# Nine adaLN products, one convolution tile, pooled sums, last squares and the last stores moved in a hybrid decoder step

## The chip, the cores and the metric

One core of one Trainium2 chip runs the whole program. The metric is the device time of one execution in microseconds (us), as the median of several runs. The engines are TensorE (PE; PEld is its loading of weights), VectorE (DVE), ScalarE (ACT), GpSimd (POOL) and SyncE (SP), which issues most of the DMAs. Each engine runs its own instructions strictly in the order in which they stand in its queue; semaphores order engines against each other.

## The reference, cut to what matters

The computation is one inference step of two layers over 1088 tokens: 1024 of a new sequence and 64 of eight running ones (eight tokens each, the "samples"). Everything is float32, the model is 1024 wide.

```
mod = silu(c) @ ada_w[i] + ada_b[i]           # adaLN: shift, scale, gate, each 1024 wide, 9 conditions
hn  = rmsnorm(x, norm_g[i]) * (1 + scale) + shift
layer 0 (SSD):  z, xbc, dt = split(hn @ w_in)             # 6176 columns
    xbc = silu(bias + causal convolution of width 4)      # x, B, C; 8 groups of 4 heads
    per chunk of 128 tokens: y = (C B^T * decay) xdt + C h * decay ;  h = decay * h + B^T xdt
    out = rmsnorm_per_group((y + d * x) * silu(z)) @ w_out
layer 1 (pool): u, z = split(hn @ w_in)                   # 2048 + 2048 columns
    pooled = windowed mean of u (2, 4, 8 or 16 tokens) - u
    out = (pooled @ w_group * scale * silu(z)) @ w_out
x = x + (1 + gate) * out                      # after each layer
y = rmsnorm(x, final_norm_g)
```

Outputs are y and the new states (SSD states, last convolution rows, last pooling rows).

## The kernel before

**Data and products.** Activations lie transposed, 128 features on the partitions and 1088 tokens beside each other, in SBUF slots that are taken and freed by hand. A float32 product is done as three products of rounded halves: `hi` = the rounded copy (ScalarE), `lo` = the rest (VectorE), and TensorE adds hi*hi, hi*lo and lo*hi (`mm1`, L190 to L192). So each weight needs a split on both engines before TensorE can use it. Weights come as a stream in a fixed list (`items`), with three raw buffers (`wr`) and two pairs of split buffers (`wh`, `wl`). `stream_next` hands out the next weight, splits the one after it and loads the following ones; raw items in between, with no split, are the adaLN weights.

**adaLN.** One adaLN block (`ada_block`, L251 to L273) is eight products of 32 columns, packed four beside each other (`am`, L261), a copy on ScalarE (`mp`) and two small selecting products one step later (L270), whose result two small VectorE instructions turn into shift and scale or gate. The first eight stand in the front stage. Fourteen more (`ada_plan`) go beside the SSD stage, and two later.

**The SSD stage** (L1587 on). Eight scans, one per group g, are cut into steps by generators, and a second generator (`beside`) yields units of projection or output products; the table `FILL` says how many units follow each scan step. Scans 0 to 3 have one unit after each of twelve steps. The steps of a scan are two fronts (transposes, C B^T), four pairs of a state step (`states`, products `S`, L623) and a row step (`rows`, products `y`, L645 and L649), where the last row step is preceded by the products Z of the samples with their old states (L664, 32 columns), then the samples' output (`back_sample`, L678), the samples' state products (`state_sample`, L700, S over 32 rows, in PSUM buffers S, y, y and tr), and the gate. The norm's sums over a group (`ms`, L763, 32 columns) and the scaling by the norm (L775) run inside the next scan, at its steps 0 and 3 (`rest`).

The units of a projection group are four weight tiles (ii = 0 to 3: B, C and two of x) of three token chunks each (c = 0 to 2). The adaLN block of a tile is opened and closed after chunks 1 and 2 for ii = 1 and 3, and after chunks 0 and 1 for ii = 2. A finished tile goes through `conv_tile`: one scaled copy on ScalarE, three taps on VectorE (L368), a tanh and two gating instructions. The last group projected is group 6, and its tile ii = 3 goes by k instead of by chunks, so that layer 0's inputs (`hn`) are freed early for the first splits (`gh`, `gl`, L805 and L806) of the output product. The first output tile (`op_first`) uses the high halves first and the low halves at its end (L835).

**The pooling layer** (L1689 on). The first two pairs of u and z tiles are plain products (`plain_pairs`, L970). Beside them `act_sums` forms sums and differences of halves of the layer's input and splits them into T1 to T4 (L1005 on ScalarE, L1006 on VectorE). The other fourteen pairs use seven products of half size instead of eight (`fast_pair`, order B11, B21, T2, T3, T1, T4, B22), with weight combinations from `w_sums`, each half split by `split_half` (L182, L184). `u_pool` forms a window's sum by repeated shifted addition (L930). After the mixing come the output products over seven block combinations in the order 2, 6, 3, 5, 1, 4, 7 (`out_product`); `block_steps` prepares the blocks of the next one (splits at L1225 and L1226, written as `b`). During product 4 the squares of finished x halves go into `ss` (L1785, L1786), and during product 7 the final norm is computed quarter by quarter, scaled (L1803 on GpSimd, L1805 on VectorE) and stored (L1806).

**What sets the order.** The program is written in the intended order, and a scheduler may bring an instruction forward on an engine when its inputs are expected earlier. `issue_after(ins)` forbids that: on the engine of `ins`, what is written in the block stands behind `ins` in the queue. It is order only, no wait between engines. The places that the change touches are of this kind, or move whole calls.

## Time and profile before

| | before |
|---|---|
| median of three runs | 1587.53 us (1587.14 to 1587.76) |
| the profiled execution's own time | 1586.18 us |
| its span | 1584.0 us |
| TensorE busy | 1568.2 us, 99% |
| VectorE busy | 1302.7 us, 82% |
| ScalarE busy | 790.8 us, 50% |
| GpSimd busy | 528.4 us, 33% |
| granted TensorE clock | 0.998 |

The profile is of one execution. Its span runs from the first to the last recorded instruction; the metric counts 2.2 us more around it. Matmuls are pipelined: the start of each is measured and its end is modelled, so two matmuls that overlap in the table are one step apart in fact, and a small wait may show as an overlap that is missing and not as idle time. "Busy" therefore says that TensorE always had something, not that it never waited.

### The profile page before, as it was taken

The numbers are of one execution on the slowest core, as the hardware profiler recorded it, in microseconds if no ns is written. First come the engines' busy times: TensorE is split into PE (matmuls) and PEld (weight loads), VectorE is DVE, ScalarE is ACT, GpSimd is POOL, SyncE is SP. The second block draws the span as 40 slices with busy tenths as digits, with TensorE's granted clock in tenths as the row PEclk, the third lists the DMA queues.
The fourth block names the chain that finished last, engine by engine and source line by source line (L and its number), as shares of the span: only waits on it lengthen the run. The fifth ranks groups of instructions, "written<-read, shape, count | busy, mean of one in ns | idle before, by whom it ended". The sixth has DMA issues, their size and how long they took to land.

```text
span 1584.0 us, 30719 instructions
## 1 busy us (share of the span) xinstructions
PE 1568.2 (99%) x11946; PEld 1504.7 (95%) x11946; DVE 1302.7 (82%) x2152; ACT 790.8 (50%) x1512; POOL 528.4 (33%) x558
## 2 busy tenths in 40 slices
PE   9999999999999999999999999999999999999997
PEld 7899999999999899989999999999999999999997
DVE  6874789887899999889888858998889777667886
ACT  6663344466666666665456338533333233233364
POOL 0133556522322413221211242576566530000241
PEclk9999999999999999999999999999999999999999
DMA  9422232355555565678999432232333379565783
GB/s 357 167 102 92 89 113 75 113 186 177 172 165 174 171 198 159 220 256 297 332 340 316 161 134 64 83 126 98 117 116 115 105 252 364 140 180 178 165 168 124
DMA packets 122304, 275.57 MB, mean 174 GB/s; under 512 B 18192, under 2 KB 59312, under 8 KB 122160
## 3 DMA queue, kind: packets, MB, share of 16 engines
q1 hardware_dynamic: 117840, 259.79, 47.9%
q0 software_dynamic: 4032, 12.72, 4.7%
q8 instruction: 94, 1.54, 0.4%
q10 hardware_dynamic: 288, 1.11, 0.2%
q14 instruction: 50, 0.41, 0.1%
HBM read 201.12 MB, written 70.23 MB: 171 GB/s over the span
## 4 chain that ended last, share of the span: by engine, by line
PE 89%; DVE 5%; issue 3%; DMA 2%; ACT 1%; POOL 0%; SPq 0%; DVEq 0%; ACTq 0%; POOLq 0%
PE st L1079 11%; PE st L1080 11%; PE st L1078 11%; PE mm L190 11%; PE mm L191 11%; PE mm L192 11%; PE op L1298 3%; PE op L1299 3%; PE op L1297 3%; PE y L645 2%; PE S L623 2%; PE y L649 2%; PE tr L584 1%; PE am L261 1%; PE tr L581 1%
## 5 line engine op out<-in xcount | busy, mean ns | idle before, releaser
L1080 PE MATMUL st<-hh,w 128*128 128x272 f32 x832 | 240.2, 289 | 0.0
L1078 PE MATMUL st<-hh,w 128*128 128x272 f32 x832 | 240.0, 289 | 0.0
L1079 PE MATMUL st<-hl,w 128*128 128x272 f32 x832 | 240.0, 288 | 0.0
L1080 PE MATMUL st<-t,w 128*128 128x272 f32 x624 | 179.6, 288 | 0.5 <-DVE w L184 0.5
L1079 PE MATMUL st<-t,w 128*128 128x272 f32 x624 | 179.3, 287 | 0.4 <-DVE t L1006 0.4
L1078 PE MATMUL st<-t,w 128*128 128x272 f32 x624 | 179.6, 288 | 0.0
L190 PE MATMUL mm<-hh,wh 128*128 128x368 f32 (+1 forms) x528 | 178.9, 339 | 0.0
L191 PE MATMUL mm<-hl,wh 128*128 128x368 f32 (+1 forms) x528 | 174.0, 330 | 0.0
L192 PE MATMUL mm<-hh,wl 128*128 128x368 f32 (+1 forms) x528 | 173.3, 328 | 0.0
L1078 PEld LDWEIGHTS st<-hh,w 128*128 128x128 f32 x832 | 156.8, 188 | 0.0
L1079 PEld LDWEIGHTS st<-hl,w 128*128 128x128 f32 x832 | 156.7, 188 | 0.0
L1080 PEld LDWEIGHTS st<-hh,w 128*128 128x128 f32 x832 | 156.4, 188 | 0.0
L182 ACT ACTIVATE w<-wr 128x512 fp32r<-128x512 f32 x104 | 65.0, 629 | 165.2 <-PE st L1080 136.2
L631 POOL TENSOR_TENSOR hd<-h,cd 128x256 f32<-128x256 f32 x56 | 46.1, 823 | 290.4 <-DVE h L632 138.4
L1297 PE MATMUL op<-b,w 128*128 128x272 f32 x448 | 129.4, 289 | 0.0
L1298 PE MATMUL op<-b,w 128*128 128x272 f32 x448 | 128.9, 288 | 0.4 <-DVE b L1226 0.4
L1299 PE MATMUL op<-b,w 128*128 128x272 f32 x448 | 129.0, 288 | 0.0
L190 PE MATMUL mm<-gh,wh 128*128 128x368 f32 (+1 forms) x372 | 125.3, 338 | 0.0
L192 PE MATMUL mm<-gh,wl 128*128 128x368 f32 (+1 forms) x372 | 122.3, 329 | 0.0
L191 PE MATMUL mm<-gl,wh 128*128 128x368 f32 (+1 forms) x372 | 122.0, 328 | 0.1
L1080 PEld LDWEIGHTS st<-t,w 128*128 128x128 f32 x624 | 117.3, 188 | 0.7 <-DVE w L184 0.7
L1079 PEld LDWEIGHTS st<-t,w 128*128 128x128 f32 x624 | 117.2, 188 | 0.6 <-DVE t L1006 0.6
(310 smaller groups left out, 4603.1 us busy)
## 6 DMA issues: line engine op xcount, KB each, us to landing
wr<-win SPq DMA_DIRECT2D x48, 512.0 KB, 3.8
wr<-pin SPq DMA_DIRECT2D x32, 512.0 KB, 3.7
acb<-acd SPq DMA_DIRECT2D x60, 256.0 KB, 5.1
wr<-pout SPq DMA_DIRECT2D x28, 512.0 KB, 3.8
x<-x1d SPq DMA_DIRECT2D x24, 544.0 KB, 6.3
x1d<-x SPq DMA_DIRECT2D x22, 544.0 KB, 4.5
wr<-pout POOLq DMA_DIRECT2D x20, 512.0 KB, 5.6
x<-xT SPq DMA_DIRECT2D x16, 544.0 KB, 8.1
```

Source lines behind the costliest of these rows:

```text
L182: self.last_hi = self.nc.scalar.activation(hi, src, AF.Copy)
L190: nc.tensor.matmul(ps[:, :n], hi[:, k, :], ah[:, a:a + n], start=first, stop=False)
L191: nc.tensor.matmul(ps[:, :n], hi[:, k, :], al[:, a:a + n], start=False, stop=False)
L192: nc.tensor.matmul(ps[:, :n], lo[:, k, :], ah[:, a:a + n], start=False, stop=last)
L623: nc.tensor.matmul(S[:, 256 * i:256 * i + 256], Bt, xde.rearrange("p r q -> p (r q)"), start=True, stop=True)
L631: nc.gpsimd.tensor_tensor(out=hd, in0=h[-1], in1=cd.unsqueeze(2).to_broadcast([P, 4, 64]), op=ALU.mult)
L1078: nc.tensor.matmul(ps[c][:, :QUART], hi[:, k], xh[:, t], start=(k == 0), stop=False)
L1079: nc.tensor.matmul(ps[c][:, :QUART], hi[:, k], xl[:, t], start=False, stop=False)
L1080: nc.tensor.matmul(ps[c][:, :QUART], lo[:, k], xh[:, t], start=False, stop=(k == 3))
L1297: nc.tensor.matmul(ps[:, :QUART], hi[:, k], xh, start=k == 0, stop=False)
L1298: nc.tensor.matmul(ps[:, :QUART], hi[:, k], xl, start=False, stop=False)
L1299: nc.tensor.matmul(ps[:, :QUART], lo[:, k], xh, start=False, stop=k == 7)
```

## The change

The change moves work between places and queues; all products stay. In its parts:

- adaLN blocks for ii = 2 open after chunk 2 of their tile and close after chunk 0 of the next tile; those for ii = 3 open after chunk 0 of the next group's first tile and close after its chunk 1. The stream's list puts the weights of the latter behind that tile's weight, and one more raw load is asked for at ii = 3.
- Group 6, tile ii = 2: taps 2 and 3 of the convolution, the tanh and the gating go behind the evictions of `back_sample`; the weight split at ii = 3 goes behind the eviction of the rows.
- The second weight pair of the output product is split behind the last `gh` and `gl`. In scan 5 the scaling by the norm (`rest`) goes from step 3 to step 4.
- Plain products: the first split of T goes behind the last weight's `hi` on ScalarE; the z tile of the second pair uses PSUM buffer tr for its first chunk. The first pooled sum's first addition goes behind the sixth half weight's low half, its second behind the last T split; for the second pooled sum the bound falls away.
- Squares in product 4 go behind the last block's split so far, on both engines.
- In the last quarter three squares are added into `ss` on VectorE and one stays for TensorE (four before). The last eight tiles are stored one by one, by turns from SP and ScalarE, in the order 5, 7, 0, 4, 1, 2, 6, 3 (four stores of two tiles from SP before).

```diff
...
                 lo = self.wp.tile([P, 8, P], F32R, tag="wl", bufs=2, name=self.name("wl"))
-            self.nc.scalar.activation(hi[:, :nk, :], raw[:, :nk, :], AF.Copy)
+            self.w_hi = self.nc.scalar.activation(hi[:, :nk, :], raw[:, :nk, :], AF.Copy).ins
...
         eng = self.nc.gpsimd if n > 6 and n % 7 in POOLW else self.nc.vector
-        eng.tensor_tensor(out=lo, in0=src, in1=hi.bitcast(F32), op=ALU.subtract)
+        self.lows.append(eng.tensor_tensor(out=lo, in0=src, in1=hi.bitcast(F32), op=ALU.subtract).ins)
...
         nc.scalar.activation(acc[:, :n], raw[:, :n], AF.Identity, bias=self.cwh[:, 128 + ti:129 + ti], scale=w[0])
+
+        def tap(k):
+            nc.vector.scalar_tensor_tensor(out=acc[:, :n], in0=raw[:, k:k + n], scalar=w[k], in1=acc[:, :n], op0=ALU.mult, op1=ALU.add)
+
+        def close():
+            nc.scalar.activation(raw[:, :n], acc[:, :n], AF.Tanh)
+            nc.vector.scalar_tensor_tensor(out=dst[:, :NP], in0=raw[:, :NP], scalar=1.0, in1=acc[:, :NP], op0=ALU.add, op1=ALU.mult)
+            th, v = (t[:, 1027:1115].rearrange("p (b w) -> p b w", w=11)[:, :, 0:8] for t in (raw, acc))
+            nc.vector.scalar_tensor_tensor(out=dst[:, NP:TOK].rearrange("p (b i) -> p b i", i=8), in0=th, scalar=1.0, in1=v, op0=ALU.add, op1=ALU.mult)
+
+        if ti == 2 * BESIDE[-1]:
+            with self.tc.issue_after(self.row_evict):
+                tap(1)
+            self.taps_late = lambda: [tap(k) for k in (2, 3)], close
+            return
         for k in range(1, 4):
-            with self.tc.issue_after(self.row_evict) if k == 1 and ti == 2 * BESIDE[-1] else contextlib.nullcontext():
-                nc.vector.scalar_tensor_tensor(out=acc[:, :n], in0=raw[:, k:k + n], scalar=w[k], in1=acc[:, :n], op0=ALU.mult, op1=ALU.add)
-        nc.scalar.activation(raw[:, :n], acc[:, :n], AF.Tanh)
-        nc.vector.scalar_tensor_tensor(out=dst[:, :NP], in0=raw[:, :NP], scalar=1.0, in1=acc[:, :NP], op0=ALU.add, op1=ALU.mult)
-        th, v = (t[:, 1027:1115].rearrange("p (b w) -> p b w", w=11)[:, :, 0:8] for t in (raw, acc))
-        nc.vector.scalar_tensor_tensor(out=dst[:, NP:TOK].rearrange("p (b i) -> p b i", i=8), in0=th, scalar=1.0, in1=v, op0=ALU.add, op1=ALU.mult)
+            tap(k)
+        close()
...
         for ii in range(4):
-            w = self.stream_next()
+            with self.tc.issue_after(self.row_evict) if (G["g"], ii) == (BESIDE[-1], 3) else contextlib.nullcontext():
+                w = self.stream_next()
+            if ii == 3 and (G["g"], 3) in self.ada_plan:
+                self.stream_raw(self.wpos + 2)
...
                         self.slots.free(*self.hn[j])
+                    if k == 0:
+                        next(self.ada_open[2], None)
...
                 return
-            ada = self.ada_do(self.ada_plan[G["g"], ii]) if (G["g"], ii) in self.ada_plan else iter(())
+            if (G["g"], ii) in self.ada_plan:
+                self.ada_open[ii] = self.ada_do(self.ada_plan[G["g"], ii])
...
                 self.proj_evict(G, ii, raw, ps, c, (G["g"], ii) != (BESIDE[-1], 2))
-                if c != (0, 0, 2, 0)[ii]:
-                    next(ada, None)
+                ada = {(1, 1): 1, (1, 2): 1, (2, 2): 2, (3, 0): 2, (0, 0): 3, (0, 1): 3}.get((ii, c))
+                if ada in self.ada_open:
+                    next(self.ada_open[ada], None)
...
                     nc.tensor.matmul(py[o, :64], xz[:, r, :], M[:, r, :64], start=True, stop=True)
-                evac_y(py, q, tok, 64)
+                evac = evac_y(py, q, tok, 64)
+            if self.taps_late:
+                taps, close = self.taps_late
+                with self.tc.issue_after(evac):
+                    taps()
+                close()
+                self.taps_late = None
...
             m -= step
-            with self.tc.issue_after(self.t_last) if p < PLAIN and step == 1 else contextlib.nullcontext():
+            with self.tc.issue_after({1: self.lows[5], 2: self.t_new}[step]) if p == 0 and step < 4 else contextlib.nullcontext():
...
         def z_tile(p, w, c, ch):
-            ps = self.pp.tile([P, 512], F32, tag="tr", bufs=2, name=self.name("pl")) if p == c == 0 else self.plain_tile(1 if p == 0 else c)
+            ps = self.pp.tile([P, 512], F32, tag="tr", bufs=2, name=self.name("pl")) if c == 0 else self.plain_tile(1 if p == 0 else c)
...
         def split(x, hi, lo):
-            nc.scalar.activation(hi, x, AF.Copy)
+            with self.tc.issue_after(self.w_hi) if not self.T else contextlib.nullcontext():
+                nc.scalar.activation(hi, x, AF.Copy)
...
             t = sl.get("t", F32R)
+            split(x, t[:, h1], t[:, h2])
             self.T[i, k] = t
-            split(x, t[:, h1], t[:, h2])
+            self.t_new = self.t_last
...
-        self.nsplit = 0
+        self.nsplit, self.lows = 0, []
...
         self.ada_late = dict(zip([(0, 4), (0, 6)], ada[len(places):]))
+        self.ada_open = {}
...
                 items.append((io["win"][6 * g + ii], 8))
-                if (g, ii) in self.ada_plan:
-                    items += self.ada_items(self.ada_plan[g, ii])
+                at = (BESIDE[BESIDE.index(g) - 1], 3) if ii == 0 and g != BESIDE[0] else (g, ii)
+                if at in self.ada_plan and (ii < 3):
+                    items += self.ada_items(self.ada_plan[at])
...
         self.acts = [[] for _ in PARTS]
-        self.zadd = None
+        self.zadd = self.taps_late = None
...
                         next(rest, None)
-                    elif i == 3 and j == 0:
+                    elif i == 3 + (g == 5) and j == 0:
...
             if d % 2 == 0:
-                ws = self.stream_pair()
+                with contextlib.ExitStack() as behind:
+                    for ins in (self.op_hi, self.op_lo) if p + d == 0 else ():
+                        behind.enter_context(self.tc.issue_after(ins))
+                    ws = self.stream_pair()
...
-        def scale(a, n, ps, groups, pool):
+        def scale(a, n, ps, groups, pool, queues=()):
...
                         nc.vector.scalar_tensor_tensor(out=t[:, i], in0=o, scalar=fg, in1=ps[:, :n], op0=ALU.mult, op1=ALU.mult)
-                nc.sync.dma_start(io["yT"][ks[0]:ks[-1] + 1][:, :, a:a + n].rearrange("k p n -> p k n"), t)
+                    if queues:
+                        queues[i % 2].dma_start(io["yT"][k][:, a:a + n], t[:, i])
+                if not queues:
+                    nc.sync.dma_start(io["yT"][ks[0]:ks[-1] + 1][:, :, a:a + n].rearrange("k p n -> p k n"), t)
...
         def squares(d, c):
-            if d and c == 0:
-                square(d, HALF, HALF)
-            if d < 3 and c == 1:
-                square(4 + d, HALF, HALF)
+            with self.tc.issue_after(self.last_block[0]), self.tc.issue_after(self.last_block[1]):
+                if d and c == 0:
+                    square(d, HALF, HALF)
+                if d < 3 and c == 1:
+                    square(4 + d, HALF, HALF)
...
         ws = ws[24:]
-        sq, sqs = [], sl.get("sq")
+        sqs = sl.get("sq")
...
                 else:
-                    t = sqs[:, QUART * d:QUART * d + QUART]
-                    nc.scalar.activation(t, x[d][:, a:a + QUART], AF.Square)
-                    sq.append(t)
+                    if d < 3:
+                        square(d, QUART, QUART)
+                    else:
+                        nc.scalar.activation(sqs[:, :QUART], x[d][:, a:a + QUART], AF.Square)
...
                             scale(0, QUART, p, ((4, 5, 6, 7), (0, 1, 2, 3)), (0, 4))
-        p1 = norm(QUART, QUART, sq)
-        scale(QUART, QUART, p1, ((4, 5), (6, 7), (0, 1), (2, 3)), (4, 6))
+        p1 = norm(QUART, QUART, [sqs])
+        scale(QUART, QUART, p1, ((5, 7, 0, 4), (1, 2, 6, 3)), (4, 6), (nc.sync, nc.scalar))
...
```

## Rows read from the trace of the kernel before

**Rows 1.** The page's busy times: us, share of the span, instructions of each engine.
```profile
PE 1568.2 (99%) x11946; PEld 1504.7 (95%) x11946; DVE 1302.7 (82%) x2152; ACT 790.8 (50%) x1512; POOL 528.4 (33%) x558
```

**Rows 2.** Stretches: from:to, length, busy PE, PEld, DVE, ACT, POOL, clock, DMA, GB/s.
```profile
481.00:553.00 72.00, 72.00 (x573) 65.79 (x572) 64.34 (x96) 48.40 (x109) 20.54 (x31) 1.00 0.54 176
...
1011.40:1053.00 41.60, 40.68 (x322) 40.24 (x321) 40.01 (x60) 15.43 (x30) 22.78 (x18) 1.00 0.40 139
```

**Rows 3.** Waits of TensorE: who, for whom: us in total, times, longest.
```profile
PE st L1080 <- DVE w L184: 0.5, 1, 0.5
...
PE st L1079 <- DVE t L1006: 0.4, 1, 0.4
PE op L1298 <- DVE b L1226: 0.4, 1, 0.4
PE pl L192 <- DVE wl L145: 0.3, 1, 0.3
```

**Rows 4.** Order of time, TensorE in op_first: start, length, what, count, idle before.
```profile
708.10 0.43 PE L835 MATMUL mm<-gl,wh 128*128 128x368 f32 x1 [0.37 <-DVE gl L806]
709.30 1.60 PE L835 MATMUL mm<-gl,wh 128*128 128x368 f32 x8 [0.77 <-DVE gl L806]
```

**Rows 5.** Order of time, TensorE around two adaLN blocks (am).
```profile
443.42 1.07 PE L261 MATMUL am<-wr,scp 128*32 128x256 f32 x16
444.42 0.44 PE L645 MATMUL y<-M,xd 128*64 128x128 f32 x4
...
759.98 1.07 PE L261 MATMUL am<-wr,scp 128*32 128x256 f32 x16
760.87 0.40 PE L664 MATMUL Z<-h,ctm 128*32 128x256 f32 x4
```

**Rows 6.** Order of time, state products of scans 1 and 4, eviction of scan 4.
```profile
482.83 0.51 PE L700 MATMUL S<-xs,Bt 32*128 32x512 f32 x4
...
696.69 1.09 PE L700 MATMUL S<-xs,Bt 32*128 32x512 f32 x4
...
695.48 0.27 DVE L615 SCALAR_TENSOR_TENSOR xbc<-xbc,vec,y 128x64 f32<-128x64 f32 x1
```

**Rows 7.** Order of time, VectorE before the last gl.
```profile
705.62 1.22 DVE L145 TENSOR_TENSOR wl<-wr,wh 128x1024 fp32r<-128x1024 f32 x1
```

**Rows 8.** Order of time in scan 5, VectorE and TensorE.
```profile
731.29 1.34 DVE L775 SCALAR_TENSOR_TENSOR xbc<-xbc,vec,rs 128x1088 f32<-128x1088 f32 x1
...
734.33 0.39 PE L645 MATMUL y<-M,xd 128*64 128x128 f32 x4
734.86 0.44 PE L649 MATMUL y<-ea,h 128*64 128x128 f32 x4
```

**Rows 9.** Order of time in the plain products, ScalarE, then VectorE.
```profile
992.03 1.75 ACT L1005 ACTIVATE t<-x 128x544 fp32r<-128x544 f32 x3
996.95 0.66 ACT L1005 ACTIVATE t<-x 128x544 fp32r<-128x544 f32 x1 [3.17 <-DVE x L1002]
997.51 1.04 ACT L141 ACTIVATE wh<-wr 128x1024 fp32r<-128x1024 f32 x1
...
1016.42 1.43 DVE L930 TENSOR_TENSOR ws<-u 128x1222 f32<-128x1222 f32 x1
```

**Rows 10.** Order of time in product 4, VectorE.
```profile
1547.79 0.73 DVE L1786 TENSOR_TENSOR ss<-ss,sq 128x544 f32<-128x544 f32 x1
1548.43 0.73 DVE L1226 TENSOR_TENSOR b<-gin,b 128x544 fp32r<-128x544 f32 x1
```

**Rows 11.** Order of time in the tail, TensorE, ScalarE, VectorE, store issues (SPq).
```profile
1573.86 2.00 PE L304 MATMUL ms<-sq,ones 128*128 128x272 f32 x8
...
1574.14 0.43 ACT L1843 ACTIVATE sq<-x 128x272 f32<-128x272 f32 x1 [1.97 <-DVE x L1282]
...
1576.85 2.54 DVE L1805 SCALAR_TENSOR_TENSOR y<-x,vec,ms 128x272 f32<-128x272 f32 x6 [2.74 <-ACT ms L1792]
...
1578.14 2.20 SPq L1806 DMA_DIRECT2D yT<-y  x4
```

**Rows 12.** GB/s of the DMAs from 1575 to 1584, in 40 slices.
```profile
GB/s 0 0 0 0 0 0 0 0 0 0 0 0 0 0 0 0 0 24 329 372 314 358 319 348 343 305 372 377 368 368 372 334 49 0 0 0 0 0 0 0
```

## The prediction

> **What bounds the kernel now.** I read the page's busy times first, then the stretches, then who waits for whom on TensorE, and last the order of time at each wait. TensorE is busy 1568.2 of the 1584.0 us span [rows 1], and a whole group of the SSD stage shows it busy 72.00 of 72.00 us [rows 2]. So no other engine's time counts as such. What can be won is of three kinds: waits of TensorE, the extra time where its tiling changes (products over 32 or 64 columns beside products over 128), and the tail behind the last product. The waits are few and short: 0.5 and 0.4 us in the pooling layer's first pair, 0.4 in the last layer's blocks, 0.3 in the plain products [rows 3]. These are idle times behind a modelled end; from start to start a wait costs more. Two low-half products start 1.20 us apart where the row gives 0.77 idle and the usual step is 0.17 (eight in 1.60, the last one's 0.43 included) [rows 4]: 1.03 lost, 0.26 more than the idle. I add 0.2 to each idle of rows 3 for that, an estimate. All the edits lie at such places, so their sum is some microseconds of 1584, and the sign is easier to tell than the size.
>
> **The change part by part** (us, against the profiled execution; minus is a gain).
>
> *Nine adaLN products moved.* No product is added or removed. Five blocks (ii = 2) go from before a scan's rows to before its sample products Z, four (ii = 3) from before the state products S to before the norm's sums one group on. A block before rows takes 1.00 from its start to that of the next product (443.42 to 444.42); the one block that stands before Z already takes 0.89 (759.98 to 760.87) [rows 5]. Z and the norm's sums both use 32 columns, so I take 0.11 for each: 9 x 0.11 = -1.0. Bounds: 0, if the product behind pays the change of tiling itself, and -1.4, if the norm's sums also save their own entry (another 0.1 on four, an estimate of the same size). Each block's two selecting products, its copy on ScalarE and its two small sums on VectorE move with it; VectorE idles 7.7 in those 72 us [rows 2]. Each block also has two weight loads on SP, and the next group's first weight now waits in SP's queue for the buffer that the moved block frees. It is needed three steps later, 18 us at 12 steps in 72 [rows 2], so I cost it at nothing; without that cover TensorE would wait for the rest of the load and for the splitting, 1.04 on ScalarE and 1.22 on VectorE [rows 7, 9], in each of four groups.
>
> *Convolution of group 6, rows before weights, second weight pair behind the last split.* Before, the sample output's eviction starts only at 695.48, behind long convolution taps, and the state products take 1.09 where the same four take 0.51 in another group [rows 6]: -0.6. The new order puts two taps behind the evictions. Then `op_first` waits for the low halves `gl`, idle 0.37 and 0.77 [rows 4], while VectorE spent 1.22 on a weight's `wl` just before them [rows 7]; the new order puts this `wl` behind both. The two gains are not independent: VectorE's queue is full here, and the end of the last `gl` sets the second wait. It comes 1.22 sooner for the `wl` and little sooner for the taps, which only change places. So both together give at least 1.2 if the queue stays as it is, and at most 0.6 + 1.5 (0.37 + 0.77 + 0.4) = 2.1; I take -1.3, near the lower end, since the queue is the nearer row. What now waits behind `wl`, the gate's second half and the norm's sum of scan 4, comes no later than before, as the `gl` leave 1.22 earlier; if one tap more gets between, the norm's sums wait, up to +0.7 (half a tap pair's 1.4, an estimate). The weight itself is wanted six products later, group 6's inputs two scans on.
>
> *Scan 5's two scalings by the norm, one step later.* Two quads of row products start 0.53 apart at 734.33, and a quad itself takes 0.39 with its drain [rows 8]; I take a usual step of 0.2, so -0.3. The state sum that they wait for is queued behind scalings of 1.34 each. These, 2.7 together, then come behind the next state sums and one unit, and evictions queue behind them; two y buffers cover that. Bounds -0.4 and +0.4 (the same wait, one step on).
>
> *Plain products and pooled sums.* Gains: the waits for the last plain weight (0.3 + 0.2), for the first pair's weight (0.5 + 0.2) and for a T half (0.4 + 0.2) [rows 3], 1.8 if all go. The last two queue on VectorE behind a pooled sum of 1.43 at 1016.42 [rows 9] and its second step; both now go behind a later weight and a later T half. The z tile in another PSUM buffer takes away a wait for an eviction, 0 to -0.3, counted as 0. Against it: the first three splits of T on ScalarE, from 992.03, now stand behind the weight's `hi`, which ran at 997.51 for 1.04. ScalarE idled 3.17 before 996.95 [rows 9]. If the `hi` runs at the start of that idle time, the splits begin at 996.95 - 3.17 + 1.04 = 994.8, 2.8 late; if it runs where it did, at 998.55, 6.5 late. I take the early place and count on VectorE forming other differences of x meanwhile, as half of them need no split; of the 2.8 I let 0.6 reach TensorE. Sum -1.2; bounds -2.1 and +7.8 (6.5, and two deferred sums of 1.43, less the 1.6 that VectorE idles in the first two pairs [rows 2]).
>
> *Last squares behind the last block's halves.* A sum of squares at 1547.79 stands ahead of a block's low half on VectorE, and the next block takes the slot that this low half frees [rows 10]; TensorE idles 0.4 for it [rows 3]: -0.6 with the 0.2. The sum comes back between there and the first norm; bounds -0.6 and +0.7 (its 0.73, if the norm's sums wait for it).
>
> *Tail.* The products over the last squares, eight matmuls, take 2.00 to 1575.86; the last square is there at 1574.14 + 0.43 = 1574.57 [rows 11]. With three of the four squares added up on VectorE, two matmuls are left behind it, one step of 0.2 and one with its drain, 0.4: 1575.2, so -0.6. Stores: before, four of two tiles each, the first issued at 1578.14, and then some 14 slices of 0.225 us at about 350 GB/s without a gap [rows 12]. The first of the six products that start at 1576.85 and take 2.54 [rows 11] is done at about 1577.3; its own store can go then, 0.8 earlier. The same bytes at the same rate end as much earlier, unless the last product, at 1579.39, holds the end; then its store is shorter by a tile of 139 KB (128 x 272 x 4 bytes), 0.4 at that rate. I take -0.5, bounds 0 and -0.8. Together -1.1.
>
> The Trainium skill (DMA: Bandwidth & Descriptors, "Issuing engines are not separate DMA queues") says that transfers of several issuing engines run interleaved on the same 16 DMA engines, so that a second issuing engine saves only the time of issuing. By this rule the second queue gives nothing once the data flow without a gap; the trace agrees, since one queue alone held 350 GB/s. By the same page ("Anatomy of one DMA") a DMA costs about 2.0 us fixed, whatever its size, and by that the stores would end 0.4 sooner and not 0.5.
>
> **Sum.** -1.0 - 1.3 - 0.3 - 1.2 - 0.6 - 1.1 = -5.5. The profiled execution took 1586.18 (the span and 2.2 around it) and would take 1580.7. The median of the runs is 1587.53, 1.35 more, and the new runs are read by their median too: 1587.5 - 5.5 = 1582.0.
>
> **The rivals.**
> *Part of it only.* A wait that goes is followed by the next late operand on the same full queue. For it: VectorE is busy 40.01 of 41.60 us in the first pairs [rows 2], and two gains have merged into one already. Against it: where VectorE idles 7.7 of 72, TensorE has no wait. Then adaLN, half the tail and a third of the other 3.4: -1.0 - 0.55 - 1.1 = -2.65, 1584.9.
> *It does not do what it says.* The new edges bind order alone; where an operand is late for a load or a buffer, the wait stays. For it: ScalarE, too, idled before it ran the weight's `hi`. Then -1.0 remains and one new wait of 0.6: 1587.1.
> *Slower.* The last plain weight's `hi` holds back the first T splits by the full 6.5, the pair's T products come late, the pooled sums fall into the next pair, and VectorE cannot make it up: +7.8 in place of -1.2, with the other -4.3 that is +3.5, 1591.0. It decides from a lateness of 3.0 on, if nothing fills VectorE meanwhile: 3.0 + 2.9 - 1.6 = 4.3, which eats the rest. Against it: that `hi` would have to run no earlier than it did.
>
> **How the numbers follow.** The forecast has 0.58 (its own range 1579.8 to 1584.3), part of it 0.23, nothing 0.10, slower 0.09. A measurement of this kernel can tell about 0.2%, 3.2 us, from no change, so faster is below 1584.4: nearly all of the forecast, 0.55, and four tenths of the second case, 0.09, together 0.64. Slower is above 1590.7: about half of the last case, 0.05. The rest, 0.31, is neither. The range for 8 in 10 begins at 1579.2, where the larger gains come near their upper bounds, and ends at 1587.2, which takes in the second case and half of the third.
>
> **What would show it.** The ii = 2 blocks stand directly before Z and take 0.89, the ii = 3 blocks before the norm's sums. The state products of scan 4 take 0.5, and the low-half products of `op_first` wait under 0.4. Scan 5's rows have no step of 0.5. The first T split starts by 995, and TensorE does not wait in the first pair. No block wait near 1550. Eight stores; two products over squares behind the norm's two instead of eight. The forecast is wrong if new waits stand between 1011 and 1053, if a row or state product waits in scans 1 to 4, or if the span is within 1 us of 1584.

## The result: slower, 1592.02 us

The changed kernel takes 1592.02 us (median of seven runs, 1591.38 to 1594.46) against 1587.14 beside it (1586.19 to 1588.12), a ratio of 1.0032, 95% interval 1.0022 to 1.0042. I had said 1582.0, and 1579.2 to 1587.2 as the range. Its profiled execution took 1592.34, with a span of 1590.6.

The page after: TensorE is as full as before [rows 1], and the work has not grown.

```profile
PE 1569.3 (99%) x11940; PEld 1508.1 (95%) x11940; DVE 1298.1 (82%) x2155; ACT 800.4 (50%) x1520; POOL 517.3 (33%) x558
```

The waits of TensorE after; the columns are who waits, for whom, us in total, times, the longest. Of [rows 3] both `st` waits and the `op` wait are gone, as forecast (the last by luck, as the squares below show). New are six waits of state products `S` for `xd`, four short ones of the samples' `S`, and the `pl` wait has grown from 0.3 to 2.9.

```profile
PE S L641 <- DVE xd L618: 4.6, 6, 2.1
PE pl L192 <- DVE wl L145: 2.9, 1, 2.9
...
PE S L724 <- DVE xbc L633: 0.7, 4, 0.2
```

**Where the time went.** I take the start of one and the same TensorE product in both traces and subtract (a plus: later than in the kernel before). The columns are the product's time in the kernel before: ahead of the scans, samples' `S` of scan 4, products `Z` of scan 5, norm's sums of scan 7 (898.46), last plain product, 2400th half product, first product of the output stage, its last one, end. The first column is from execution to execution; what counts are differences along a row. Even these carry the execution: e8 and e12 have the same instructions in the same order on every engine up to 950, and e12 alone has a wait of 0.7 ahead of the first output product. The experiments' rows come from their profiled executions in the same way.

```
                      343.4  696.7  760.9  898.5 1011.4 1061.2 1403.1 1573.3 1584.0
changed               -0.38   3.49   1.92   5.10   9.94   8.49   8.48   7.58   6.57
e1  adaLN undone      -0.04   0.22   0.70   2.49   7.48   6.03   6.02   5.12   4.11
e2  scan 5 undone     -0.36   4.53   3.61   3.61   5.80   5.75   5.74   4.83   3.82
e3  T order undone    -0.71   3.37   1.80   3.92   3.88   3.44   3.43   2.55   1.55
e4  all three undone   0.11   0.03   1.08   1.08   1.06   0.63   0.62  -0.29  -0.73
e5  adaLN alone        0.11   4.05   2.08   2.08   2.08   2.08   2.08   1.56   1.58
e6   + other bank      0.17   2.97   2.02   2.02   1.93   1.93   1.92   1.33   1.35
e7   + evict first    -0.49   0.95  -0.07  -0.07  -0.06  -0.03  -0.04  -0.70  -0.70
e8   + both           -0.76  -0.50  -2.55  -2.55  -2.63  -2.60  -2.61  -3.39  -3.38
e9  conv. alone       -0.52  -0.05  -0.20  -0.10  -0.13  -0.11  -0.12  -0.41  -0.40
e10 pair alone        -0.64   0.12   4.20   4.20   4.17   4.18   4.16   3.49   3.49
e11 changed + copy    -0.24   3.57   2.20   2.82   4.88   4.79   4.77   4.29   3.29
e12 best              -0.61  -0.21  -1.54  -1.54  -1.64  -2.07  -2.08  -2.82  -3.83
e13 T order + sums    -0.47  -0.69  -0.61  -0.61   3.08   1.63   1.61   1.11   1.11
e14 sums alone         0.05   0.09   0.65   0.65   0.70   0.25   0.24  -0.46  -0.45
```

The changed kernel loses 3.9 in scans 0 to 3, gains 1.6 to 760.9, loses 3.2 in scan 7 and 4.8 in the plain products, then gains 1.5, 0.9 and 1.0.

**Scans 0 to 3, first wait.** TensorE and VectorE of the changed kernel at the samples of scan 0 (start, duration, engine, line, operation, tiles, count, idle before and its releaser):

```profile
409.43 0.49 PE L724 MATMUL S<-xs,Bt 32*128 32x512 f32 x2
410.10 0.50 PE L724 MATMUL S<-xs,Bt 32*128 32x512 f32 x2 [0.18 <-DVE xbc L633]
```

```profile
408.03 0.26 DVE L633 SCALAR_TENSOR_TENSOR xbc<-xbc,vec,y 128x64 f32<-128x64 f32 x1
408.49 1.23 DVE L372 SCALAR_TENSOR_TENSOR xbc<-raw,raw 128x1024 f32<-128x1024 f32 x1 [0.20 <-ACT raw L371]
409.63 0.22 DVE L374 SCALAR_TENSOR_TENSOR xbc<-raw,raw 128x64 f32<-128x64 f32 x1
409.77 0.28 DVE L633 SCALAR_TENSOR_TENSOR xbc<-xbc,vec,y 128x64 f32<-128x64 f32 x1
```

The second pair of `S` starts 0.67 behind the first (0.01 is usual) and at the end of the second eviction, 410.05, which frees its PSUM buffer. The waits table shows only 0.2 of this as idle. The same places in the kernel before:

```profile
409.65 0.46 DVE L615 SCALAR_TENSOR_TENSOR xbc<-xbc,vec,y 128x64 f32<-128x64 f32 x2
```

```profile
410.20 1.07 PE L261 MATMUL am<-wr,scp 128*32 128x256 f32 x16
411.20 0.51 PE L700 MATMUL S<-xs,Bt 32*128 32x512 f32 x4
```

The second eviction ended no earlier there, at 410.11, and `S` began behind the block, at 411.20. But the block was not needed for that: the two evictions stand together there, and the second ends 0.09 ahead of the block's start (0.08 in scans 1 and 3; in scan 2 it ends 0.33 behind it). What is new is VectorE's order. In the kernel before the gating stands behind both evictions, at 411.23; in the changed kernel it is ready earlier, and its 1.23 and 0.22 stand between them. By these rows the block's 1.0 would have covered that (409.43 + 1.00 is behind 410.05), but with the old order its absence would have cost at most 0.33, in scan 2.

**Second wait.** At the next scan's start, changed kernel (TensorE, then VectorE):

```profile
419.26 1.07 PE L261 MATMUL am<-wr,scp 128*32 128x256 f32 x16
420.15 0.64 PE L787 MATMUL ms<-z,ones 128*32 128x272 f32 x8
...
426.43 0.38 PE L602 MATMUL tr<-kc,xbc 128*128 128x128 f32 x2
...
430.47 0.67 PE L641 MATMUL S<-xd,Bt 128*128 128x256 f32 x2 [0.42 <-DVE xd L618]
```

```profile
425.88 0.36 DVE L295 TENSOR_SCALAR gat<-am,adab 128x9 f32<-128x9 f32 x2
...
429.64 0.68 DVE L618 TENSOR_TENSOR xd<-tr,tkx 128x512 f32<-128x512 f32 x1
```

The block's `am` lies in one of the two PSUM buffers `tr` (L258) from 419.26 until VectorE has read it, at 426.24. The next scan's transposes need both buffers; the second set comes only at 426.43, its `xd` ends at 430.32, and `S` waits: 0.74 from the start of the product ahead of it to its own, where 0.2 is usual (0.57 in the sums below, against the 0.17 of a plain product).

**Scan 7.** ScalarE, then TensorE, of the changed kernel:

```profile
862.89 0.21 ACT L627 ACTIVATE cd<-acb 128x4 f32<-128x4 f32 x1 [2.09 <-DMA acb<-acd]
863.01 1.05 ACT L141 ACTIVATE wh<-wr 128x1024 fp32r<-128x1024 f32 x1
863.96 1.26 ACT L610 ACTIVATE M<-acb,tka 128x128 f32<-128x128 f32 x4
...
865.65 0.25 ACT L606 ACTIVATE Bt<-tr 128x128 f32<-128x128 f32 x1
```

```profile
866.97 0.67 PE L641 MATMUL S<-xd,Bt 128*128 128x256 f32 x2 [2.08 <-DVE xd L618]
```

ScalarE waits 2.09 for a load that only the next chunk needs; this chunk's copy `Bt`, and by it `xd`, stand behind. The step at `S` is 2.45 where 0.22 is usual, 2.2 of the 3.2.

**Plain products.** ScalarE's high half of the last plain weight is done at 1000.58. VectorE (second fence) then takes five differences of x, and the low half only at 1004.84, in 2.28 where 1.22 is usual. The third fence is TensorE, the fourth the stretches with the granted clock (PEclk).

```profile
999.52 1.06 ACT L141 ACTIVATE wh<-wr 128x1024 fp32r<-128x1024 f32 x1 [0.74 <-PE pl L191]
```

```profile
1000.56 1.35 DVE L1026 TENSOR_TENSOR x<-x,x 128x544 f32<-128x544 f32 x2
1001.83 0.71 DVE L1026 TENSOR_TENSOR x<-x 128x544 f32<-128x544 f32 x1
1002.46 0.71 DVE L1026 TENSOR_TENSOR x<-x,x 128x544 f32<-128x544 f32 x1
1003.21 1.70 DVE L1026 TENSOR_TENSOR x<-x 128x544 f32<-128x544 f32 x1
1004.84 2.28 DVE L145 TENSOR_TENSOR wl<-wr,wh 128x1024 fp32r<-128x1024 f32 x1
```

```profile
1003.94 0.33 PE L191 MATMUL pl<-hl,wh 128*128 128x368 f32 x1
1007.17 0.68 PE L192 MATMUL pl<-hh,wl 128*128 128x368 f32 x1 [2.90 <-DVE wl L145]
1007.64 0.51 PE L190 MATMUL pl<-hh,wh 128*128 128x368 f32 x1
```

```profile
core 0: us, PE busy (x) PEld busy (x) DVE busy (x) ACT busy (x) POOL busy (x), PEclk, DMA share, GB/s
...
1004.00:1007.20 3.20, 0.30 (x3) 0.03 (x1) 3.20 (x3) 0.42 (x1) 3.12 (x3) 0.85 0.00 0
1007.20:1010.00 2.80, 2.80 (x9) 2.80 (x10) 2.80 (x3) 1.08 (x2) 2.41 (x3) 0.50 0.00 0
1010.00:1013.00 3.00, 3.00 (x11) 3.00 (x11) 2.96 (x6) 1.53 (x4) 0.00 (x0) 0.50 0.38 49
1013.00:1016.00 3.00, 3.00 (x19) 3.00 (x18) 1.15 (x2) 0.48 (x1) 0.00 (x0) 0.99 0.84 337
```

After the step of 3.23 TensorE's clock is at its lower level (0.50, that is 1.2 of 2.4 GHz) until about 1013: products start 0.307 apart and not 0.169, 19 of them, 2.6 more. Of the wait itself about 1.1 is the low half's own length (2.28 for 1.22), while GpSimd is busy 3.12 of 3.20 us; in e3 the same low half takes 1.21. That GpSimd slows it is not shown.

**Tail**, answering to [rows 11] (TensorE, VectorE, and the store queues of SP and ScalarE):

```profile
1582.20 0.73 PE L304 MATMUL ms<-sq,ones 128*128 128x272 f32 x2 [0.60 <-ACT sq L1880]
```

```profile
1583.92 2.54 DVE L1836 SCALAR_TENSOR_TENSOR y<-x,vec,ms 128x272 f32<-128x272 f32 x6 [2.23 <-ACT ms L1823]
```

```profile
1584.44 2.81 SPq L1838 DMA_DIRECT2D yT<-y  x4
```

```profile
1585.21 1.87 ACTq L1838 DMA_DIRECT2D yT<-y  x4
```

From the last output product to the first scaling it is 3.06 (before 3.57), from there to the end 6.68 (before 7.15). In e4, with the same tail, the second time is 7.2: its eight stores, the first issued as early, follow one another at other times and end no earlier than the four of the kernel before.

### The profile page after: what moved, and what is told of

Same layout as the page of the kernel before. It is cut to its first block, busy times and chain, and to the rows that moved or that the text cites. A ratio compares the mean times of both kernels' runs of the same rounds, so it can differ in the third digit from the quotient of the medians.

```text
span 1590.6 us, 30729 instructions
## 1 busy us (share of the span) xinstructions
PE 1569.3 (99%) x11940; PEld 1508.1 (95%) x11940; DVE 1298.1 (82%) x2155; ACT 800.4 (50%) x1520; POOL 517.3 (33%) x558
## 4 chain that ended last, share of the span: by engine, by line
PE 85%; DVE 7%; issue 3%; ACT 3%; DMA 2%; POOL 0%; SPq 0%; DVEq 0%; ACTq 0%; POOLq 0%
PE st L1106 11%; PE st L1104 11%; PE st L1105 11%; PE mm L190 9%; PE mm L191 9%; PE mm L192 9%; PE op L1323 4%; PE op L1325 4%; PE op L1324 4%; DVE raw L368 2%; PE S L641 2%; PE y L663 2%; PE y L667 1%; DMA acb<-acd 1%; PE tr L602 1%
```

## The experiments

Ratios are to the kernel before on the same chip, with 95% intervals. A single time (e6, e7, e9, e10) says little, since runs of the kernel before on one chip lie up to 6.3 us apart; there the trace decides.

**e1 to e4: one part undone, then three.**

```diff
 e1 (also the stream's list and its extra load, as before)
-                ada = {(1, 1): 1, (1, 2): 1, (2, 2): 2, (3, 0): 2, (0, 0): 3, (0, 1): 3}.get((ii, c))
+                if c != (0, 0, 2, 0)[ii]:
+                    next(ada, None)
 e2
-                    elif i == 3 + (g == 5) and j == 0:
+                    elif i == 3 and j == 0:
 e3
-            with self.tc.issue_after(self.w_hi) if not self.T else contextlib.nullcontext():
 e4: all three
```

> The changed kernel with the nine adaLN blocks back in their old places (and the stream's list as before); everything else as changed. Theory A (three separate losses): the block that stood before a scan's sample state products covered the eviction that they wait for; in its new place it covers nothing, and each of the scans 0 to 3 loses 0.66 there and 0.57 at the first state products of the next scan, less 0.11 twice. So these eight waits go, the waits at 864.5 and 1003.9 of the changed kernel stay, and the time is 1592.0 - 3.5 = 1588.5. Rival (the later stages lose because they start 3.5 later against the loads): the wait near 864 goes as well, 1585.5 or less. Rival (the moved blocks do gain 1.0, as I predicted, and the eight waits come from another part): 1593.

Measured 1587.75 against 1586.65, 1.0008 (0.9999 to 1.0017). The eight waits are gone (343.4 to 696.7: +0.26 instead of +3.87); those in scan 7 (a step of 1.79) and in the plain products stay. So theory A, not the lateness.

> The changed kernel with scan 5's scaling by the norm back at step 3; everything else as changed. Theory A: moving it one step made the order of loads and of ScalarE's work in scans 5 to 7 another one, in which scan 7's front waits for a load of decay values (the step from 864.51 takes 2.45 us, where the usual one takes 0.22); with it back that wait goes, the scan-5 row step of 0.42 comes back, and the time is 1592.0 - 3.0 + 0.4 = 1589.4. Rival (scan 7 waits because TensorE and the loads have shifted against each other, whatever scan 5 does): the wait near 864 stays, 1592.0 to 1592.4.

1589.29 against 1586.65, 1.0014 (1.0005 to 1.0023). From 760.9 to 898.5 nothing is lost (3.2 in the changed kernel), though scan 7 starts later than there. In scan 5 the move had been worth 0.7 (a gain of 0.4 here to 760.9 from the norm's sums of scan 4, of 1.1 there). So the move caused scan 7's wait.

> The changed kernel without the order that puts the first split of T behind the last plain weight's high half on ScalarE; everything else as changed. Theory A: that order made VectorE take seven differences of x (0.71 each, 1.7 beside GpSimd) ahead of the weight's low half, which is ready to be formed at 1000.6 and runs at 1004.8 to 1007.1; TensorE waits 3.06 for it, and the 19 products after that run at half the clock (0.306 apart where 0.169 is usual: 2.6 more). Without it the low half runs right behind the high half, the wait falls to the 0.5 that the kernel before has, the clock stays at 1.0, and the time is 1592.0 - 3.06 - 2.6 + 0.5 = 1586.8. Rival (the low half is late because GpSimd's weight sums slow VectorE in that stretch, whatever the order): TensorE still waits over 2 there, 1590 to 1592.

1587.42 against 1586.65, 1.0004 (0.9995 to 1.0013). The step at the low half is 1.01 instead of 3.23, and the clock stays up; nothing is lost from 898.5 to 1011.4.

> The changed kernel without those three parts: the adaLN blocks, scan 5's scaling and the first T split stand as in the kernel before; the convolution, the second weight pair, the pooled sums, the z tile's buffer, the last squares and the tail as changed. Theory A (the three losses are separate and all else gains): 1587.1 - 1.6 (convolution and low halves) - 1.2 (two T waits of 0.66 and 0.58) - 0.8 (squares) - 1.1 (tail) = 1582.4. Rival (every move makes the scheduler place other work anew, and new waits come in their stead): 1585 or more, with waits of over 0.5 in scans 5 to 7 or in the plain products.

1584.38 against 1586.65, 0.9983 (0.9974 to 0.9992): faster, but by 2.3 and not by 4.7. The rival has a part: a wait of 1.6 for ScalarE's eviction ahead of the first output product, 1.1 for `xd` in scan 5, and 0.9 near 1049 for a low half on GpSimd.

**e5 to e8: the adaLN blocks alone, and what hangs on their places.**

```diff
 e6, e8: blocks opened at (0, 0)
-        pm = self.pp.tile([P, 512], F32, tag="tr", bufs=2, name=self.name("am"))
+        pm = self.pp.tile([P, 512], F32, tag=self.am_tag, bufs=2, name=self.name("am"))   # "y"
 e7, e8: the gating of tile ii = 2 in scans 0 to 3, in back_sample
-                evac_y(py, q, tok, 64)
+                evac = evac_y(py, q, tok, 64)
+            if self.close_late:
+                with self.tc.issue_after(evac):
+                    self.close_late()
```

> The kernel before with the nine adaLN blocks moved as in the change, and nothing else of it. Theory A: this alone costs what scans 0 to 3 lose in the changed kernel, four times (0.66 at the samples' state products + 0.57 at the next scan's first state products - 2 x 0.11) = +4.0, so about 1591 against 1587, and TensorE reaches the state products of scan 4's samples 3.9 later than in the kernel before. Rival (the blocks' move costs nothing by itself; the waits need the other parts): 1586, 1.0 below the kernel before.

1587.76 against 1585.92, 1.0010 (1.0000 to 1.0019). To 696.7 it loses 3.94, as expected; 2.0 of it comes back to 760.9, where the waits of [rows 4] and the 0.59 at scan 4's samples are gone. That I had not seen: the changed positions help there; why is not shown.

> As e5, but the blocks that are opened ahead of the norm's sums use a PSUM buffer of y instead of one of tr. Theory A for the second wait: such a block holds one of the two tr buffers from its opening until VectorE has read its last product (419.3 to 426.2 in the changed kernel), and the next scan's transposes, which stood right behind the norm's sums before, come only at 426.4, so the first state products wait 0.57 for VectorE's xd. With another buffer the transposes come ahead again and the four waits of 0.57 go: 2.3 below e5; the four of 0.66 at the samples' state products stay. Rival (VectorE's order makes xd late, not the buffer): as e5.

1587.11 (one run). The four waits of 0.57 fall to 0.2 (a step of 0.37); the transposes stand right behind the norm's sums again (TensorE, e6):

```profile
419.81 1.07 PE L263 MATMUL am<-wr,scp 128*32 128x256 f32 x16
420.70 0.64 PE L773 MATMUL ms<-z,ones 128*32 128x272 f32 x8
421.27 0.49 PE L591 MATMUL tr<-xbc,xbc 128*128 128x128 f32 x2
...
430.67 0.67 PE L633 MATMUL S<-xd,Bt 128*128 128x256 f32 x2
```

To 696.7 only 1.1 of the 2.3 is saved: the buffer's share of each wait is 0.37, 1.5 in all, and the samples' steps of scans 1 and 3 grow by 0.2. What the other 0.2 of each wait hangs on is not shown.

> As e5, but in scans 0 to 3 the last two gating instructions of the convolution (1.23 and 0.22 on VectorE) stand behind the samples' two evictions instead of between them. Theory A for the first wait: the samples' state products need the PSUM buffer that the second eviction frees; it ends at 410.04 behind the 1.23 of the gating; the adaLN block of 1.0 that stood there before covered that. With the evictions first the four waits of 0.66 go: 2.6 below e5; the four of 0.57 stay. Rival (TensorE's own order or the operand xs is late there, from ScalarE): as e5.

1585.07 (one run). All four waits of 0.66 are gone, the others stay; 2.5 saved to 696.7. Its order, both evictions ahead of the gating, is that of the kernel before. So VectorE's order makes this wait: without the gating between the evictions the block is not missed.

> As e5, with both of these edits. Theory A: all eight waits go and what is left is the saving in tiling that I predicted for the moved blocks, 4.0 - 2.3 - 2.6 = -0.9 against the kernel before (-0.1%), with TensorE about 1.0 earlier at scan 4's samples. Rival (other operands are late right behind these two, since VectorE's and ScalarE's queues have not become shorter): half or more of the 4.0 stays.

1583.59 against 1585.92, 0.9984 (0.9975 to 0.9994). The four waits of 0.66 are gone, and of the other four 0.2 each is left. To 696.7 the move costs 0.26 instead of 3.94, and it keeps the 2.0 behind it: with both repairs the moved blocks gain 1.8 in all up to 760.9. The two causes account for the loss; the gain to 696.7 that I had predicted (0.9) is not there, as those four times 0.2 eat most of it; the gain behind it is larger. No run has the repairs without the move.

**e9, e10: convolution part alone; second weight pair alone** (each the change's own lines, as above).

> The kernel before with the convolution part alone: group 6's last two taps, tanh and gating behind the samples' evictions, and the weight split at ii = 3 behind the rows' eviction. Theory B: the wait of 0.59 at scan 4's sample state products goes as I predicted, but a new one takes its place, TensorE's first output product waits for ScalarE's eviction of group 6's last tile (1.6 to 1.8 in e1 and e4, where the adaLN blocks also stand in their old places); TensorE is 1.0 to 1.2 later at that product than in the kernel before. Rival (the 1.6 comes from the second weight pair's new place): TensorE is 0.6 earlier there.

1585.36 (one run; before 1586.44). Theory B is wrong for it: no wait for an eviction. The 0.59 at scan 4's samples goes, the first low-half wait grows from 0.39 to 0.82, and from 696.7 to 760.9 it gains 0.15.

> The kernel before with the second weight pair of the output product split behind the last gh and gl, and nothing else. Theory B: the waits for the low halves (0.39 and 0.89 beyond a usual step) fall to about 0.9 together, but the weight's low half (1.22 on VectorE) now stands directly ahead of the first operands of scan 5, whose first state products wait 1.1 for xd: TensorE is 0.5 to 0.7 later in scan 5. Rival (my prediction's step: nothing that is wanted soon is queued behind that low half): 0.7 to 1.2 earlier.

1589.64 (one run). The state products wait 1.1 for `xd`, queued behind the weight's low half, as theory B says (VectorE, then TensorE, e10):

```profile
709.80 1.21 DVE L145 TENSOR_TENSOR wl<-wr,wh 128x1024 fp32r<-128x1024 f32 x1
...
711.13 0.68 DVE L600 TENSOR_TENSOR xd<-tr,tkx 128x512 f32<-128x512 f32 x1
```

```profile
711.96 0.67 PE L623 MATMUL S<-xd,Bt 128*128 128x256 f32 x2 [0.94 <-DVE xd L600]
```

But the loss from 696.7 to 760.9 is 4.1: the samples' step grows to 1.04, and in scan 5 a row step takes 2.48 (0.42 before). The state sum that it needs stands behind two scalings with convolution taps between them, as in the kernel before; new is that VectorE waits 2.46 (0.48 before) for the load that the first scaling needs. SP issues it behind a weight's load, at 725.23; in the kernel before it stands ahead of that weight, at 721.30 (VectorE, then SP, e10):

```profile
731.35 1.35 DVE L775 SCALAR_TENSOR_TENSOR xbc<-xbc,vec,rs 128x1088 f32<-128x1088 f32 x1 [2.46 <-DMA rs<-rsd]
```

```profile
723.69 0.38 SPq L119 DMA_DIRECT2D wr<-wout  x1
725.23 0.32 SPq L771 DMA_DIRECT2D rs<-rsd  x1
```

The sign is theory B's, the size is not.

**e11: scan 7's order on ScalarE alone.**

```diff
+            behind = (lambda: self.tc.issue_after(self.front_copy)) if g == 7 and c > 1 else contextlib.nullcontext
             if 0 < c < 8:
-                nc.scalar.activation(ea, acb, AF.Exp)
+                with behind():
+                    nc.scalar.activation(ea, acb, AF.Exp)
...
+                with self.tc.issue_after(before) if g == 7 and c > 1 else contextlib.nullcontext():
+                    nc.scalar.activation(cd, acb[:, :, 127], AF.Exp)
```

> The changed kernel with one edit: in scan 7, from chunk 2 on, a chunk's exponentials of its decay (ea and cd on ScalarE) stand behind the copy of B of the chunk before. All other engines' orders are the same. Theory A for scan 7: at 862.9 ScalarE waits 2.1 for the load of chunk 4's decay, for its cd; chunk 3's copy of B, ready to be made, stands behind it and behind a weight's 1.04 and four masks, and TensorE's state products wait for the xd that follows it (the step of 2.45 at 864.51). With the copy ahead that step falls below 0.7 and the time by 1.8 to 2.3, to 1589.7 to 1590.2 (against 1587.1). Rival (chunk 3's own data are late): the step stays above 2.

1588.49 against 1586.44, 1.0015 (1.0006 to 1.0024). ScalarE's copy is made at 862.53, no wait stands in scan 7, and from 760.9 to 898.5 it loses 0.6 instead of 3.2. In the plain products it loses 2.8 less as well, since the clock stayed at 1.00 behind the same wait; 1.3 of that is lost again at 1049 (ScalarE, then TensorE, e11):

```profile
862.53 0.26 ACT L608 ACTIVATE Bt<-tr 128x128 f32<-128x128 f32 x1
```

```profile
864.09 1.02 PE L644 MATMUL S<-xd,Bt 128*128 128x256 f32 x4
```

**e13, e14: the plain products' orders alone** (the change's own lines).

> The kernel before with the first T split behind the last plain weight's high half and the pooled sums' new order, nothing else. Theory A: the order alone makes the wait, whatever the scans do: TensorE's step at the first wl of the second pair's z tile is 3.2 (0.64 in the kernel before), 2.6 lost; the two T waits (0.66 and 0.58) go and up to 1.0 of them comes back near 1049 on GpSimd's low half. So +1.3 to +2.4 where the clock stays at 1.0. If the fall of the clock comes in some executions only, those are 2.7 longer, and the times lie in two groups. Rival (the wait needs the scans' lateness): as e14.

1588.51 against 1586.60, 1.0010 (1.0001 to 1.0019). The step is 3.24 without any lateness of the scans, so the order alone makes it; 3.7 are lost to 1011.4: 2.6 by the wait and 1.5 by a lower clock (11 products at 0.307), less 0.4 gained ahead of them.

> The kernel before with the pooled sums' new order alone. Theory A: the T waits of 0.66 and 0.58 go, -1.2, and GpSimd's low half near 1049 takes 0.9 of it back: -0.3, within what can be told from no change. Rival (my prediction: nothing is late behind them): -1.3 and no wait near 1049.

1585.42 against 1586.60, 0.9994 (0.9985 to 1.0003). Theory A: 1.45 gained to 1036, 1.0 of it lost at 1049:

```profile
PE st L1081 <- POOL w L184: 0.7, 1, 0.7
```

**e12: what the runs point to**: e8 with the pooled sums, last squares and tail of the change.

> What the runs point to: the kernel before with the adaLN blocks moved and both of e8's repairs, the pooled sums', the last squares' and the tail's part of the change; not the convolution, the second weight pair, scan 5's scaling, the first T split and the z tile's buffer. Theory A: e8's gain (2.6 up to the pooling layer's products) + 1.25 for two T waits, of which up to 1.0 is given back near 1049 where GpSimd's low half is late + 0.9 for the tail + 0 to 0.6 for the squares: 3.8 to 5.4 below the kernel before, a ratio of 0.9966 to 0.9976. Rival (gains do not add, since VectorE's queue carries lateness from one part to the next): no faster than e8, 0.9984.

1581.94 against 1586.44, 0.9969 (0.9956 to 0.9981), faster than both kernels and in the middle of what theory A gave. Beside the start's, its largest wait in the waits table is 0.7 us. Up to 760.9 it gains 0.9 where e8 gained 1.8, and the intervals of the two overlap: that it is faster than e8 is not shown.

## Why the prediction was wrong, step by step

*adaLN: predicted -1.0, measured +3.9 to scan 4's samples.* The step "so I take 0.11 for each" priced the tiling, and where a block stands before `Z` the tiling came out so: it takes 0.89 (542.20 to 543.09). What failed is the step that put all else at nothing with "VectorE idles 7.7 in those 72 us", for idle time says nothing of a queue's order or of a buffer. Without the block in its place the gating came between two evictions (e7, 0.66 in each scan), and in its new place the block holds a PSUM buffer that the next scan needs (e6, 0.37 in each). The first is the very wait that the prediction meant to take away in scan 4. It took the eviction at 695.48 [rows 6] for the late one; the state products wait for the second, behind a tap (kernel before, VectorE):

```profile
695.67 1.37 DVE L368 SCALAR_TENSOR_TENSOR raw<-raw,cwh,raw 128x1112 f32<-128x1112 f32 x1
696.96 0.27 DVE L615 SCALAR_TENSOR_TENSOR xbc<-xbc,vec,y 128x64 f32<-128x64 f32 x1
```

Four equal waits, one in each scan, might have pointed to the buffer: the Trainium skill (Perfetto Trace Analysis, "Optimization Strategy") says that the same gap repeating on the engine that should be full can mean too little SBUF or PSUM for the next tile. The trace agrees: the step of 0.74 came four times, and another PSUM buffer brought it down to 0.37.

*Convolution and second pair: -1.3; -0.5 measured from scan 4's samples to the norm's sums (3.49 to 3.02).* But the blocks' move alone gives -1.6 there (e5, 4.05 to 2.44), so these two parts cost 1.1 in the changed kernel, and 1.5 and 1.7 where the blocks stand in their old places (e4, e1). The 0.59 at the samples went, as it does in e5. "What now waits behind `wl` [...] comes no later than before" failed: I listed the gate and the norm's sum, and not `cb` and `xd` of the next scan's front. In the changed kernel `xd` costs the full 1.09 there. By itself the second pair's move loses 4.1 (e10), the convolution's gains 0.15 (e9).

*Scan 5's scalings: -0.3; about -0.7 in scan 5, but +3.2 in scan 7.* The sign in scan 5 was luck. The wait of 0.3 at 734.86 belongs to that execution: up to there e13 and e14 have the order of the kernel before on every engine, and it is 0 in e13 and 0.65 in e14. The 0.7 is another thing. Without the move (the kernel before and eleven experiments) an adaLN block of scan 5 runs in two pieces with projection products between, with it (the changed kernel, e1, e3, e11) in one; the changed kernel gains 0.8 just there, from 2.70 late to 1.92 (TensorE before, then changed):

```profile
738.32 1.05 PE L261 MATMUL am<-wr,scp 128*32 128x256 f32 x10
...
741.50 0.63 PE L261 MATMUL am<-wr,scp 128*32 128x256 f32 x6
```

```profile
742.97 1.07 PE L261 MATMUL am<-wr,scp 128*32 128x256 f32 x16
```

What no step of mine held is that the scheduler places the following scans' work anew: the loads' and ScalarE's order differ up to scan 7, and there a head of ScalarE's queue waits for a load (e2, e11).

*Plain products: -1.2; +4.8 - 1.5.* "I take the early place and count on VectorE forming other differences of x meanwhile" failed. The high half did come early, and VectorE did form those differences, ahead of the very low half that TensorE needs next. The lateness of 2.8 that the prediction weighed did not come: the order holds one T split, and others ran ahead of the high half, the first at 997.10, 5.1 behind 992.03 where TensorE is 4.8 to 5.1 behind. My slower rival had the right edge and the wrong victim: it named the T products, and it was the weight. The wait costs 2.6, the lower clock behind it 2.6 here. The two T waits went as predicted; in e2, e3, e4, e11, e12 and e14 0.9 to 1.3 of that came back on GpSimd, the merging that the case "part of it only" held.

*Last squares: -0.6; -0.9 in the changed kernel, but not the change's.* The wait ahead of 1550.66 is gone as well in e5, e8, e10 and e14, which don't have the edit (-0.5 to -0.8), and still there in e9. From 1100 on e9 and e14 have the order of the kernel before on every engine, so a wait of single executions had been read as a fixed one.

*Tail: -1.1; -1.0,* in the changed kernel and in e1, e2, e3, e11 and e12: 0.5 by the squares and 0.5 by the stores, of 0.6 and 0.5. In e4 the squares give 0.5 and the stores nothing, though the first is issued as early. So "the same bytes at the same rate end as much earlier" does not hold of itself; what decides it is not shown, and no run tells the second queue from the storing tile by tile.

By the table the parts sum to +6.6 of span. The medians differ by 4.9: the profiled execution of the kernel before took 1.0 less than its median and that of the changed kernel 0.3 more, and outside the span lie 1.7 instead of 2.2.

**Open.** What decides whether the clock falls, and how long it stays low, is not settled: after the same step of 3.23, e2 and e11 show 1.00 throughout, e13 loses about 1.5 us, the changed kernel 2.6 and e1 2.8.

## What to carry to other kernels

Before you move a piece of work off a full engine's path, ask what the other engines' queues do without it: what is ready earlier there may land between two instructions that the full engine waits for, and the price of that is not the piece's own time. List what it holds from start to end (a PSUM buffer, a queue place), and go through every instruction that lands behind a moved one until the next front. Where a scheduler places the rest, take one part at a time and compare the start of the same product along the trace, for the loss may stand two scans on. A wait of some tenths in a single trace may be that execution's own: two of those aimed at here were gone, or larger, in runs with the same queue orders.

## What the runs showed of the hardware

After one wait of 2.9 us the granted clock fell to 0.50 for some 6 us in the changed kernel, and in e2 it did not, with the same wait (granted 1.00 from 1000 to 1015). In e1 it fell, too. A wait of 2.1 in scan 7 left it at 1.00. A wait for a PSUM buffer shows mostly as a longer step and little as idle time: 0.67 from start to start beside 0.18 idle.
